# Local attention of a decoder trunk: one narrow split product for the meta keys, exponentials as a step of their own, output projection opened with three of four operand tiles

## The chip, the cores and the metric

The kernel runs on one NeuronCore of a Trainium2 chip. The core has five engines with a queue each: PE (TensorE, matrix products; its weight loads are listed apart as PEld), DVE (VectorE), ACT (ScalarE), POOL (GpSimd) and SP (which here issues transfers from memory). PE writes its results to eight banks of PSUM; everything else lives in SBUF, 128 partitions wide. The metric is the device time of one execution in microseconds (us); less is better.

## The reference

Two layers over 512 tokens and 16 meta tokens ahead of them, 1024 wide, all in float32. Layer 0 mixes by gated linear attention, layer 1 by local attention; each mixer stands between two half-step feed-forward nets, and each of these parts between two RMS norms. The change touches the local attention of layer 1, cut here to what matters:

```python
def swa_mixer(hn, w_q, sinks, w_out, k, v, cos, sin):
    q = (hn @ w_q).reshape(B, L, N_KV_HEADS, GROUP, HEAD_DIM)          # 4 key heads x 4, 64 wide
    q = apply_partial_rope(q, cos, sin) * (HEAD_DIM ** -0.5)
    ...
    k_band, v_band = band(k), band(v)       # per block of 128: 16 meta keys, the block before, the block itself
    s = jnp.einsum('bkgnqd,bknsd->bkgnqs', q_blk, k_band)
    mask = [meta: always, block before: j > i and blk > 0, own block: j <= i]
    p = sink_softmax(s, mask, sink_b)       # the sink adds exp(sink - max) to the denominator
    o_real = jnp.einsum('bkgnqs,bknsd->bkgnqd', p, v_band)
    ...
    return o @ w_out
...
hn = rmsnorm(h, g[2]); mix = swa_mixer(...); h = h + rmsnorm(mix, g[3])
```

The keys and values are made once, after layer 0, and shared (`shared_kv`). The meta positions are dropped from the output.

## The kernel before, in words

All activations are kept transposed: 1024 features as 8 tiles of 128 partitions, tokens along the free axis, in two groups of 256 (`L1`) or all 512 at once (`L1W`). Weights come from memory as plain float32 in 256 KB pieces and are split on chip: ACT copies a tile to the type fp32r (high part), DVE subtracts that copy from the original (low part). A product of two split operands is three products, high x high, low x high, high x low (`mm3s`, lines 348 to 359). A product of unsplit float32 operands is one instruction in the program and two records in the trace. `pair` tiles (32 slots of 2 x 528 elements per partition) hold weights, operands and most intermediates.

**Order.** The order of PE is the order in which the program calls it, and that is written by a small planner, `Flow` (lines 75 to 127). It keeps a clock that each product advances by an estimate (`mm`, line 175: columns/2400 us for split operands, columns/600 for plain ones). Jobs are generators; what they yield is a delay in planner time or another job to wait for. After a split product with a pump (`flow.pump()` in `mm3s`) all jobs that are due emit their instructions. With four outputs at once, as in `x_first`, the pumps stand at the last four of each twelve products; with one output, behind every third. The delays are constants at the top of the file.

**Local attention** (`swa`, from line 1250). One visit handles a pair of heads over two query blocks; 16 visits (`visits`) run as two jobs each. `soft(i)`: score products `sa` and `sb` for 4 (head, block) pairs, copy to SBUF (ACT, L1328), masked insertion of the block before (DVE, L1330), the sink's column (L1346), maximum (L1347), its scaling (L1348), four exponentials with row sums (ACT, L1350); after `SOFT` the reciprocal (L1355), the 16 meta weights of both heads scaled into `mt` (L1360) and the 128 others scaled in place (L1363). `core(i)`: `NORM` later two transposes of `mt` (`ptm`), copied to the tile `pm` (L1376), and four of the others (`pt`, L1384 and L1386); `PROBS` later the output bank `o`: one plain float32 product for the meta keys over 32 rows (two heads x 16), then products of 64 x 128 for the others (`vt`, `dv`); then `split` into the operand tile `so[u]` (L451, L452). `pace` keeps visits at least `PERIOD` (first eight) or `SLOWER` apart, and visit i waits for the core of visit i - 5.

Between the visits PE runs work from outside them: the second half of the query projection (`x`), and the output projection (`y`, `out_steps`, from line 666). The latter runs in two halves of four operand tiles `so`; for each group of 256 tokens and each of 8 output tiles `begin` makes the products with the first three operand tiles and `unit` adds the fourth and hands the bank on. For the second group it first waits for the visits of that group (`second`).

**Behind the attention**, `Residual.run` (per group): after a delay plus `sums[gi]` the sums of squares go through `root` on PE and DVE (`st_post`), after `DCHAIN` plus `factors[gi]` a product spreads the factors over the partitions (`r_post`, from the tile `dg_post`, L426), and DVE and ACT add the residual and build the next operand's tiles (L525, L526, L474, L475). The next net starts with `x_first`: four weight tiles at once, 96 products for group 0, then 96 for group 1, tile by tile as they are built. `fin` for the attention is made at line 1530.

**Shared values** (`shared_kv`, from line 1198): `place` transposes V into `vt`, forms the differences `dv` and the two tiles `vmz`, which hold the 16 meta rows of two value heads, each zero in the other head's rows (`rowm` is the 0/1 mask).

Of the kernel before, what the change touches and what calls it, by code (L numbers as in the profile page):

```python
# [11 lines left out]
I32 = mybir.dt.int32  # L12
# [31 lines left out]
SCORE = 0.8  # L44
SOFT = 6.5
ADDED = 1.4
LONGER = 0.8
BEHIND = 2.2
NORM = 4.0
BUSY = 2.6  # L50
# [5 lines left out]
SQUARES = 6.0  # L56
SLACK = 1.0
LAG = 5
PERIOD = 3.1
SLOWER = 3.6  # L60
GATHER = 1.5
# [77 lines left out]
def trunk_kernel(ctx: ExitStack, tc, a, out, last_out):  # L139
# [21 lines left out]
    def pair_tile(name, dt=F32R):  # L161
        return hp.tile([P, 2, TOK], dt, tag="pair", name=name)
# [5 lines left out]
    def flat(t):  # L168
        return t.rearrange("p a t -> p (a t)")
# [496 lines left out]
    def out_steps(hid, groups, split_groups, first, finish=None, tailm=0, packed=False, jobs=(), second=(), late=1):  # L666
# [80 lines left out]
        for gi, g in enumerate(split_groups):  # L747
            if gi:
                flow.wait(*second)
            for m in range(KD - tailm, KD):  # L750
                if finish and finish.turned(gi) and m == KD - 2:
                    hold(KD - 1, g)
                unit(m, g)
                if finish:
                    sq(m, gi)
                if gi:
                    done_w(through(m) - freed)
                    freed = through(m)
            if finish:
                flow.spawn(finish.run(gi, g, accs[gi]))  # L760
# [437 lines left out]
    def shared_kv(x, kp, behind):  # L1198
        kz = [kp.tile([P, 4, META + P], F32, name=f"kz{j}") for j in range(2)]
        vt = flat(pair_tile("vt", F32))[:, :1024].rearrange("p (b v) -> p b v", v=256)  # L1200
        dv = flat(pair_tile("dv", F32))[:, :768].rearrange("p (b v) -> p b v", v=256)
        vmz = [t[:, :P] for t in duo("vmz")]
        rowm = kp.tile([P, 8], F32, name="rowm")
        sp.dma_start(rowm, a["rowmask"])
# [16 lines left out]
        def place(drained):  # L1221
# [3 lines left out]
            for j in range(2):  # L1225
# [9 lines left out]
                vm = duo(f"vm{j}")[0]  # L1235
                dve.tensor_copy(vm[:, :32].rearrange("p (e m) -> p e m", m=META), v[:, :META].unsqueeze(1).to_broadcast([P, 2, META]))
                yield 1.0
                p = ps(f"vmT{j}")
                transpose(p[:32, :P], vm[:, :32])
                for e in range(2):  # L1240
                    d = slice(64 * e, 64 * e + 64)
                    dve.tensor_tensor(vmz[j][:32, d], p[:32, d], rowm[:32, e : e + 1].to_broadcast([32, 64]), op=ALU.mult)
                yield 1.0
            dve.tensor_tensor(dv, vt[:, 1:], vt[:, :3], op=ALU.subtract)

        job = flow.spawn(place(x_first(x, 4, evac, behind=behind, first_ahead=6)))
        return (kz, vt, dv, vmz), job


    def swa(x, kv, finish):  # L1250
        kz, vt, dv, vmz = kv
        cap[0] = used[0] + 8
        with tc.tile_pool(name="ap", bufs=1) as ap:
            mgt = ap.tile([P, P], I32, name="mgt")
            sp.dma_start(mgt, a["mgt"])
            mle = ap.tile([P, P], F32, name="mle")
            sp.dma_start(mle, a["mle"])
# [4 lines left out]
            sp.dma_start(sr, a["sinp"])  # L1262
            sel = ap.tile([P, 32], F32, name="sel")
            sp.dma_start(sel, a["sel"])
# [42 lines left out]
            def soft(i, after_jobs):  # L1307
# [39 lines left out]
                dve.tensor_reduce(nm, s, axis=AX.X, op=ALU.max, negate=True)  # L1347
                dve.tensor_tensor(pairs(nm), pairs(nm), both(rc), op=ALU.mult)  # L1348
                for c in range(4):
                    act.activation(  # L1350
                        s[:, c], s[:, c], AF.Exp, scale=rc[:, c % 2 : c % 2 + 1], bias=nm[:, c : c + 1],
                        accum_out=den[:, c : c + 1],
                    )
# [3 lines left out]

                mt = sm.tile([P, 2, 2, META], F32, tag="mt", name=f"mt{u}_{hf}", bufs=3)
                pairs = lambda t: t.rearrange("p (e c) m -> p e c m", c=2)
                dve.tensor_tensor(  # L1360
                    mt.rearrange("p c e m -> p e c m"), pairs(s[:, :, :META]), pairs(rd.to_broadcast([P, 4, META])), op=ALU.mult
                )
                dve.tensor_tensor(s[:, :, META:144], s[:, :, META:144], rd.to_broadcast([P, 4, P]), op=ALU.mult)  # L1363
                probs[i] = s, mt

            def core(i):
# [6 lines left out]
                for c in range(2):  # L1373
                    transpose(pm[:32, c * P : (c + 1) * P], mt[:, c].rearrange("p e m -> p (e m)"))
                ptm = sm.tile([32, 256], F32, tag="ptm", name=f"pm{u}_{hf}", bufs=2)
                act.activation(ptm, pm[:32, :256], AF.Copy)  # L1376
                p = ps(f"pt{u}_{hf}")
# [12 lines left out]
                kvh = [slice((2 * j + e) * 64, (2 * j + e) * 64 + 64) for e in range(2)]  # L1390
                mm(o[:, :256], vmz[j][:32], ptm, True, True)
                for c in range(2):
# [119 lines left out]
    with tc.tile_pool(name="kp", bufs=1) as kp:  # L1512
# [17 lines left out]
        nxt, fin = into("l1f1", 1, 3, False, lambda k: gain(1, 4, k), L1, post=(2, 2))  # L1530
        fin.sums[0] = SLACK
        flow.wait(placed)
# [18 lines left out]
def _layout(x, meta_tokens, norm_gains, w_ffn_in, w_ffn_out, gla_w_in, gla_w_gate, gla_b_gate, gla_norm,  # L1551
# [75 lines left out]
```

## Time and profile before

| | |
|---|---|
| median of 3 runs | 1878.34 us (1878.25 to 1880.12) |
| profiled execution, its own time | 1879.77 us |
| its span, first to last instruction | 1878.0 us |
| mean granted clock of TensorE | 0.998 |
| PE, PEld busy | 1867.2, 1786.4 us |
| DVE, ACT, POOL busy | 1398.1, 1026.7, 164.1 us |
| local attention, first score product to the last o product | about 1393 to 1498 us |

Times in rows are from the start of the span. A row of a group of instructions gives line, engine, operation, `out<-in` by tile names, partitions x elements and type; count; behind the bar busy us and mean ns of one; behind the second bar the idle time of the engine just before them and what ended it. A row in order of time gives start, length, engine, line and operation, merged over equal neighbours, with idle time in brackets. Matmul records overlap in their tails, so the cost of one is read from start to start. A row of the view of stretches gives busy time and instruction count of each engine, then the granted clock (1.00 is full speed), the share of the 16 DMA engines and GB/s.

### The profile page before, as it was taken

The page shows a single profiled execution, that of the slowest core. Times are in us where ns is not written, and L with a number is a line of the kernel's source. Part 1 is how long each engine was busy: PE and PEld are TensorE (multiplying, and loading weights), DVE is VectorE, ACT ScalarE, POOL GpSimd, SP SyncE. Part 2 cuts the span into 40 slices and gives each one's busy share as a digit, 9 for nine tenths or more (in the row PEclk, how much of TensorE's full clock was granted, in tenths as well). Part 3 has the DMA queues.
Part 4 walks back from the last instruction along what each step waited for, and adds up shares of the span by engine and source line. Part 5 has one row for each costly group of instructions (what it writes and reads, how often), then busy time and mean ns, then how long its engine had stood idle before and what let it go on. Part 6 is the DMA issues. An engine that isn't in the chain of part 4 may idle for free.

```text
span 1878.0 us, 37247 instructions
## 1 busy us (share of the span) xinstructions
PE 1867.2 (99%) x14463; PEld 1786.4 (95%) x14463; DVE 1398.1 (74%) x2837; ACT 1026.7 (55%) x2309; POOL 164.1 (9%) x295
## 2 busy tenths in 40 slices
PE   9999999999999999999999999999999999999998
PEld 9999999999999999999999898989988898989898
DVE  7885858767564788585887886868777679858685
ACT  5663635654446566363674553535767756636364
POOL 2000000330001300000033000000320140000002
PEclk9999999999999999999999999999999999999999
DMA  5233333421213123232351223233421212333331
GB/s 175 95 97 99 93 105 96 138 69 57 66 60 113 46 91 105 88 105 92 103 174 46 73 86 112 92 111 98 140 74 52 69 46 73 101 103 104 102 113 60
DMA packets 102274, 174.70 MB, mean 93 GB/s; under 512 B 11857, under 2 KB 24017, under 8 KB 102097
## 3 DMA queue, kind: packets, MB, share of 16 engines
q1 hardware_dynamic: 101664, 171.74, 28.8%
q8 instruction: 113, 1.85, 0.4%
q10 hardware_dynamic: 432, 0.59, 0.1%
q14 instruction: 65, 0.52, 0.1%
HBM read 169.66 MB, written 2.10 MB: 91 GB/s over the span
## 4 chain that ended last, share of the span: by engine, by line
PE 91%; DVE 6%; ACT 1%; issue 1%; DMA 0%; SPq 0%; DVEq 0%; ACTq 0%
PE y L176 31%; PE x L176 20%; PE a L176 19%; PE c L176 8%; PE d L176 5%; PE o L176 1%; DVE raw L265 1%; ACT w_s L259 1%; DVE w_s L260 1%; PE e L176 1%; DVE w L260 1%; PE po L176 1%; PE sa L176 1%; PE pt L188 1%; DVE w L241 1%
## 5 line engine op out<-in xcount | busy, mean ns | idle before, releaser
L260 DVE TENSOR_TENSOR w_s<-raw,w_s 128x512 fp32r<-128x512 f32 x288 | 193.9, 690 | 129.3 <-ACT w_s L259 127.2
L176 PE MATMUL y<-hidl0f,w 128*128 128x256 f32 (+1 forms) x2112 | 262.4, 285 | 1.1 <-DVE hidl0f L452 0.9
L176 PEld LDWEIGHTS y<-hidl0f,w 128*128 128x128 f32 x2112 | 259.3, 188 | 2.2 <-DVE hidl0f L452 1.5
L241 DVE TENSOR_TENSOR w<-raw,w 128x512 fp32r<-128x512 f32 x376 | 235.7, 655 | 30.1 <-ACT w L240 27.9
L259 ACT ACTIVATE w_s<-raw 128x512 fp32r<-128x512 f32 x288 | 175.1, 628 | 150.7 <-DVE raw L265 137.4
L176 PE MATMUL y<-hidl1f,w 128*128 128x512 f32 (+1 forms) x1344 | 251.1, 346 | 0.3
L176 PEld LDWEIGHTS y<-hidl1f,w 128*128 128x128 f32 x1344 | 212.4, 188 | 35.1 <-DVE hidl1f L941 1.5
L240 ACT ACTIVATE w<-raw 128x512 fp32r<-128x512 f32 x376 | 207.2, 586 | 39.8 <-PE y L176 29.9
L265 DVE TENSOR_TENSOR raw<-raw,raw 128x512 f32<-128x512 f32 x288 | 198.1, 688 | 5.5
L446 POOL TENSOR_TENSOR acc_post<-acc_post,sq_post 128x256 f32<-128x256 f32 (+1 forms) x77 | 62.6, 812 | 1532.4 <-ACT sq_post L445 1531.3
L260 DVE TENSOR_TENSOR w<-raw,w 128x512 fp32r<-128x512 f32 x216 | 148.4, 688 | 29.8 <-ACT w L259 29.0
L259 ACT ACTIVATE w<-raw 128x512 fp32r<-128x512 f32 x216 | 134.1, 621 | 41.6 <-PE y L176 41.0
L176 PE MATMUL x<-x_l0m,w 128*128 128x272 f32 (+1 forms) x1152 | 152.0, 288 | 0.0
L176 PEld LDWEIGHTS x<-x_l0m,w 128*128 128x128 f32 x1152 | 143.3, 188 | 2.7 <-issue 1.7
L705 DVE TENSOR_TENSOR Y<-y,Y 128x256 f32<-128x256 f32 (+2 forms) x175 | 82.0, 474 | 73.3 <-PE y L176 72.8
L176 PE MATMUL a<-zl0f_t,w_s 128*128 128x264 f32 x864 | 117.1, 285 | 0.0
L176 PE MATMUL a<-zl1f_t,w_s 128*128 128x256 f32 x864 | 114.7, 282 | 0.5 <-ACT c L916 0.4
L176 PEld LDWEIGHTS a<-zl0f_t,w_s 128*128 128x128 f32 x864 | 109.9, 188 | 0.3
L176 PEld LDWEIGHTS a<-zl1f_t,w_s 128*128 128x128 f32 x864 | 107.4, 188 | 2.4 <-ACT c L916 2.0
L176 PE MATMUL x<-x_l0f,w 128*128 128x256 f32 (+1 forms) x768 | 98.0, 287 | 0.8 <-DVE w L241 0.8
L176 PEld LDWEIGHTS x<-x_l0f,w 128*128 128x128 f32 x768 | 94.9, 188 | 2.0 <-DVE w L241 1.5
L176 PE MATMUL x<-x_l1f,w 128*128 128x256 f32 (+1 forms) x576 | 94.4, 323 | 0.0
(513 smaller groups left out, 3221.1 us busy)
## 6 DMA issues: line engine op xcount, KB each, us to landing
raw<-in_w_in SPq DMA_DIRECT2D x352, 256.0 KB, 2.9
raw<-in_w_out SPq DMA_DIRECT2D x96, 256.0 KB, 3.2
raw<-in_w_last SPq DMA_DIRECT2D x48, 256.0 KB, 3.1
raw<-in_gla_in SPq DMA_DIRECT2D x48, 256.0 KB, 3.2
raw<-in_w_out SPq DMA_DIRECT2D x64, 128.0 KB, 2.8
raw<-in_gla_out SPq DMA_DIRECT2D x16, 256.0 KB, 2.8
raw<-in_w_q SPq DMA_DIRECT2D x16, 256.0 KB, 4.5
raw<-in_swa_out SPq DMA_DIRECT2D x16, 256.0 KB, 3.0
```

The lines of the kernel that those rows point to most:

```text
L176: inst = pe.matmul(o, lhs, rhs, start=start, stop=stop, skip_group_check=onto)
L188: pe.transpose(o, src, ident)
L240: act.activation(w[:, 0, :m], raw[:, :m], AF.Copy)
L241: dve.tensor_tensor(w[:, 1, :m], raw[:, :m], w[:, 0, :m].bitcast(F32), op=ALU.subtract)
L259: act.activation(w[:, 0, :512], src, AF.Copy)
L260: dve.tensor_tensor(w[:, 1, :512], src, w[:, 0, :512].bitcast(F32), op=ALU.subtract)
L265: dve.tensor_tensor(dst, dst, src, op=ALU.add)
L446: pool.tensor_tensor(sums[0][:, :n], sums[0][:, :n], t[:, :n], op=ALU.add)
L705: dve.tensor_tensor(y, p[:, :n], y, op=ALU.add)
```

## The change

- The meta product becomes one split product over 96 rows. `mt` grows from 2 x 32 to 3 x 32 columns per block: the third part is first the plain weight (`mf`), ACT copies it to the first two parts as fp32r (high), and after `HIGH` DVE turns the third into the low part. The transposes `ptm` give 96 rows instead of 32, copied to an fp32r tile. On the value side `vmz` gets 96 rows: high, low, high (built in `place`, with the mask of two columns).
- The exponentials are issued `LARGEST` = 1.5 after the maximum; `SOFT` goes from 6.5 to 4.6, `NORM` from 4.0 to 2.5 with `HIGH` = 1.5 ahead of it.
- `PERIOD` 3.1 to 2.8, `SLOWER` 3.6 to 3.1.
- In the output projection of the attention, `begin` is called for the first two output tiles of each group before the first is finished (`OPENED`; only where `second` is given).
- Behind the attention `sums[0]` = 1.0 is dropped and `factors[1]` = 1.8 (`CROWDED`) set.
- The tables `mgt`, `mle` and `sel` move from a pool of their own into the unused end of the tile that holds `dv`.

```diff
-SOFT = 6.5
+LARGEST = 1.5
+SOFT = 4.6
...
-NORM = 4.0
+HIGH = 1.5
+NORM = 2.5
...
+OPENED = 2
+CROWDED = 1.8
 LAG = 5
-PERIOD = 3.1
-SLOWER = 3.6
+PERIOD = 2.8
+SLOWER = 3.1
...
             if gi:
                 flow.wait(*second)
+
+            for m in range(KD - tailm, KD - tailm + (OPENED if second else 0)):
+                begin(m, g)
             for m in range(KD - tailm, KD):
...
-        dv = flat(pair_tile("dv", F32))[:, :768].rearrange("p (b v) -> p b v", v=256)
-        vmz = [t[:, :P] for t in duo("vmz")]
-        rowm = kp.tile([P, 8], F32, name="rowm")
+        dv = flat(pair_tile("dv", F32))
+        dv, spare = dv[:, :768].rearrange("p (b v) -> p b v", v=256), dv[:, 768:]
+        both = pair_tile("vmz")
+        vmz = [both[:, j, :P] for j in range(2)]
+        rowm = kp.tile([P, 2], F32, name="rowm")
...
-                dve.tensor_copy(vm[:, :32].rearrange("p (e m) -> p e m", m=META), v[:, :META].unsqueeze(1).to_broadcast([P, 2, META]))
+                dve.tensor_copy(vm[:, :96].rearrange("p (e m) -> p e m", m=META), v[:, :META].unsqueeze(1).to_broadcast([P, 6, META]))
                 yield 1.0
                 p = ps(f"vmT{j}")
-                transpose(p[:32, :P], vm[:, :32])
+
+                transpose(p[:96, :P], vm[:, :96])
+                zm = duo(f"zm{j}")[0][:96, :P]
                 for e in range(2):
                     d = slice(64 * e, 64 * e + 64)
-                    dve.tensor_tensor(vmz[j][:32, d], p[:32, d], rowm[:32, e : e + 1].to_broadcast([32, 64]), op=ALU.mult)
+                    dve.tensor_tensor(zm[:, d], p[:96, d], rowm[:96, e : e + 1].to_broadcast([96, 64]), op=ALU.mult)
+                act.activation(vmz[j][:96], zm, AF.Copy)
+                dve.tensor_tensor(vmz[j][32:64], zm[32:64], vmz[j][32:64].bitcast(F32), op=ALU.subtract)
...
-            mgt = ap.tile([P, P], I32, name="mgt")
+            mgt = spare[:, :P].bitcast(I32)
             sp.dma_start(mgt, a["mgt"])
-            mle = ap.tile([P, P], F32, name="mle")
+            mle = spare[:, P : 2 * P]
             sp.dma_start(mle, a["mle"])
...
-            sel = ap.tile([P, 32], F32, name="sel")
+            sel = spare[:, 2 * P :]
             sp.dma_start(sel, a["sel"])
...
                 dve.tensor_tensor(pairs(nm), pairs(nm), both(rc), op=ALU.mult)
+
+                yield LARGEST
                 for c in range(4):
                     act.activation(
                         s[:, c], s[:, c], AF.Exp, scale=rc[:, c % 2 : c % 2 + 1], bias=nm[:, c : c + 1],
...
-                mt = sm.tile([P, 2, 2, META], F32, tag="mt", name=f"mt{u}_{hf}", bufs=3)
+                mt = sm.tile([P, 2, 3, 32], F32R, tag="mt", name=f"mt{u}_{hf}", bufs=3)
                 pairs = lambda t: t.rearrange("p (e c) m -> p e c m", c=2)
+                mf = mt[:, :, 2].bitcast(F32)
                 dve.tensor_tensor(
-                    mt.rearrange("p c e m -> p e c m"), pairs(s[:, :, :META]), pairs(rd.to_broadcast([P, 4, META])), op=ALU.mult
+                    mf.rearrange("p c (e m) -> p e c m", m=META), pairs(s[:, :, :META]), pairs(rd.to_broadcast([P, 4, META])), op=ALU.mult
                 )
+                act.activation(mt[:, :, :2], mf.unsqueeze(2).to_broadcast([P, 2, 2, 32]), AF.Copy)
                 dve.tensor_tensor(s[:, :, META:144], s[:, :, META:144], rd.to_broadcast([P, 4, P]), op=ALU.mult)
+                yield HIGH
+                dve.tensor_tensor(mt[:, :, 2], mf, mt[:, :, 0].bitcast(F32), op=ALU.subtract)
                 probs[i] = s, mt
...
-                    transpose(pm[:32, c * P : (c + 1) * P], mt[:, c].rearrange("p e m -> p (e m)"))
-                ptm = sm.tile([32, 256], F32, tag="ptm", name=f"pm{u}_{hf}", bufs=2)
-                act.activation(ptm, pm[:32, :256], AF.Copy)
+                    transpose(pm[:96, c * P : (c + 1) * P], mt[:, c].bitcast(F32).rearrange("p r k -> p (r k)"))
+                ptm = sm.tile([96, 256], F32R, tag="ptm", name=f"pm{u}_{hf}", bufs=2)
+                act.activation(ptm, pm[:96, :256], AF.Copy)
...
-                mm(o[:, :256], vmz[j][:32], ptm, True, True)
+                mm(o[:, :256], vmz[j][:96], ptm, True, True)
...
-        fin.sums[0] = SLACK
+        fin.factors[1] = CROWDED
         flow.wait(placed)
         swa(x, kv, fin)
...
-    c["rowmask"] = (i // META == np.arange(8)[None, :]).astype(np.float32)
+    c["rowmask"] = (i // META % 2 == np.arange(2)[None, :]).astype(np.float32)
```

More of the change, by code (lines that the diff above doesn't have):

```diff
@@ L1246, in shared_kv @@
         job = flow.spawn(place(x_first(x, 4, evac, behind=behind, first_ahead=6)))
-        return (kz, vt, dv, vmz), job
+        return (kz, vt, dv, vmz, spare), job
     def swa(x, kv, finish):
-        kz, vt, dv, vmz = kv
+        kz, vt, dv, vmz, spare = kv
         cap[0] = used[0] + 8
         with tc.tile_pool(name="ap", bufs=1) as ap:
-            mgt = ap.tile([P, P], I32, name="mgt")
+            mgt = spare[:, :P].bitcast(I32)
             sp.dma_start(mgt, a["mgt"])
-            mle = ap.tile([P, P], F32, name="mle")
+            mle = spare[:, P : 2 * P]
             sp.dma_start(mle, a["mle"])
```

## The prediction

> **What bounds the kernel now.** I read the page first, then who waited for whom, then the stretch that the change touches.
>
> ```profile
> PE 1867.2 (99%) x14463; PEld 1786.4 (95%) x14463; DVE 1398.1 (74%) x2837; ACT 1026.7 (55%) x2309; POOL 164.1 (9%) x295
> PE 91%; DVE 6%; ACT 1%; issue 1%; DMA 0%; SPq 0%; DVEq 0%; ACTq 0%
> ```
>
> PE is busy for 99% of the span and is 91% of the chain that ended last: time is won by giving PE less to do or by closing one of its few gaps. The view of waits for PE names the gaps, longest first:
>
> ```profile
> PE r_post_l1f L176 <- DVE dg_post_l1f L426: 2.0, 1, 2.0
> PE busy L1442 <- DVE eps L1494: 1.0, 1, 1.0
> ```
>
> The longest, 2.0 us, lies just behind the local attention. Inside it there is none, by busy time in its stretch (columns: us, then PE, PEld, DVE, ACT, POOL busy with counts, clock, DMA share, GB/s):
>
> ```profile
> 1400.00:1498.00 98.00, 98.00 (x877) 80.90 (x875) 69.85 (x186) 77.53 (x245) 4.75 (x6) 1.00 0.21 65
> ```
>
> So a product made cheaper here pays in full as long as ACT (77.5 of 98) and DVE (69.9) keep up.
>
> **The meta product.** PE in order of time (start, length, line, operation, count):
>
> ```profile
> 1443.39 3.44 PE L176 MATMUL y<-so,w 128*128 128x256 f32 x27
> 1446.77 0.69 PE L176 MATMUL o<-pm,vmz 32*128 32x256 f32 x2
> 1447.39 0.44 PE L176 MATMUL o<-pt,vt 128*64 128x128 f32 x4
> ...
> 1449.33 4.18 PE L176 MATMUL y<-so,w 128*128 128x256 f32 x33
> 1453.35 0.38 PE L188 MATMUL ptm<-ident,mt 128*32 128x128 f32 x2
> ...
> 1455.01 2.04 PE L176 MATMUL y<-so,w 128*128 128x256 f32 x15
> 1456.88 0.38 PE L188 MATMUL ptm<-ident,mt 128*32 128x128 f32 x2
> ```
>
> The product over the 16 meta keys is plain f32 and stands as two records: 1447.39 - 1446.77 = 0.62 us from its start to the next. A split (fp32r) product of the same 256 columns is a y: 33 of them take 4.02 (1449.33 to 1453.35) and 15 take 1.87, so one costs (4.02 - 1.87)/18 = 0.119 and the entry into such a block about 0.09. The block of 27 ends in a plain product and takes 3.38, 0.08 more than 27 x 0.119 + 0.09: leaving the block costs 0.08, and the change only shifts that behind the meta product. So where the meta product follows a split one it saves 0.62 - 0.119 = 0.50. In the timeline 12 of the 16 do (as here; the first of them at 1422.21, the last at 1496.42); the other 4 follow transposes or score products and would need entry and exit of their own: 0.50 - 0.17 = 0.33. Sum: 12 x 0.50 + 4 x 0.33 = **7.3 us**. Bounds for what the trace does not show, a split product over 96 rows: no gain at all if it costs what the plain one does (0), and 16 x 0.50 = 8.0. I take 7.3, since the y product has the same columns and 128 rows.
>
> The Trainium skill (FP8 and Floating Point Precision, TensorE Precision Notes) counts true fp32 as four passes through the array. As an estimate from that, three passes of 0.119 are saved, 0.36 a product and 5.7 in all in place of 7.3; the trace has 0.62 in two records, more than four such passes, so the row decides.
>
> The transposes that feed it load 96 columns instead of 32:
>
> ```profile
> 1433.84 0.38 PE L188 MATMUL ptm<-ident,mt 128*32 128x128 f32 x2
> 1434.06 0.60 PE L188 MATMUL pt<-ident,s 128*128 128x128 f32 x4
> 1434.41 1.67 PE L176 MATMUL y<-so,w 128*128 128x256 f32 x12
> ```
>
> Two with 32 columns take 0.22, four with 128 take 0.35: about 0.1 each either way, so 96 columns cost nothing.
>
> **What ACT and DVE get in return.** Groups of the stretch 1400 to 1498:
>
> ```profile
> L1350 ACT ACTIVATE s<-s,nm,roots 128x145 f32<-128x145 f32 x48 | 23.8, 498 | 8.3 <-DVE nm L1348 8.2
> L1376 ACT ACTIVATE pm<-ptm 32x256 f32<-32x256 f32 x16 | 5.8, 363 | 1.7 <-PE ptm L188 1.7
> L1384 ACT ACTIVATE pt<-pt 128x512 f32<-128x512 f32 x16 | 9.3, 580 | 0.2
> L445 ACT ACTIVATE sq_post<-Y 128x256 f32<-128x256 f32 x6 | 2.4, 410 | 1.5 <-DVE Y L705 1.5
> L1360 DVE TENSOR_TENSOR mt<-s,den 128x64 f32<-128x64 f32 x12 | 2.7, 227 | 0.3
> ```
>
> New on ACT is one copy of 128 elements a visit. From 256 to 512 elements a copy grows by 580 - 363 = 217 ns, so 128 fewer than L445's 256 is 410 - 109 = 0.30 us; bounds half of L445's and all of it, 0.2 and 0.41. 16 x 0.30 = 4.8 us. New on DVE is one subtraction of 64 elements: by L1360 0.23, at most twice that, 16 x 0.23 = 3.7. The stretch shrinks to 98 - 7.3 = 90.7; ACT then has 82.3 (91%), DVE 73.6 (81%). Against that, ACT stood idle for 8.2 us ahead of L1350, the exponentials at the head of its queue waiting for the maximum of their own visit; issued 1.5 later in the planner's time, they let other copies go ahead. Two waits are new: ACT's copy for DVE's weights, behind which the next copies of scores and transposes queue, and DVE's subtraction for that copy, behind which the next maximum and the weight splits queue; the 1.5 ahead of the subtraction is longer than the copy's 0.30. Cover for the additions is that idle time; without it, 4.8 is what ACT falls behind. I book 0.5 us for one gap as small as those already in the list of waits, between 0 and 3.
>
> **Pace.** Visits start 0.3 (later 0.5) sooner after one another, and from exponentials to transposes the plan goes from 6.5 + 4.0 = 10.5 to 1.5 + 4.6 + 1.5 + 2.5 = 10.1. The tightest visit I found:
>
> ```profile
> 1431.38 0.68 DVE L1363 TENSOR_TENSOR s<-s,den 128x512 f32<-128x512 f32 x1
> ```
>
> The scaled weights are there at 1432.06, their transposes run at 1434.06: 2.0 to spare, against 0.4 less plan and 0.23 more DVE. Cost 0.
>
> **Edits at nothing.** Two tiles opened with three of four operands: the order of 9 products changes, not their number; a second bank is held some 9 x 0.119 = 1.1 us longer. The row below (1498.07) shows no wait there to remove. The table loads leave their own pool for the spare end of dv:
>
> ```profile
> L1255 SPq DMA_DIRECT2D mgt<-in_mgt x1: 328/328/328, 17.1 to 17.1; - x1
> L1264 SPq DMA_DIRECT2D sel<-in_sel x1: 861/861/861, 18.4 to 18.4; - x1
> ```
>
> They now go out 17 us into the kernel, where their place was free; in a slot that others use first they can't, so these three issues (0.33, as much again for mle, and 0.86: 1.5 us on SP) move late in SP's queue, past most weight loads, and what is queued behind them waits for that slot. Weights lie ahead in a ring, so I book 0, at most 1.5. Preparing the wider meta values adds two small copies on ACT and some four subtractions or wider multiplications' worth on DVE, about 0.6 and 0.9 us, in a stretch with room and PE full:
>
> ```profile
> 1025.00:1040.00 15.00, 15.00 (x93) 13.19 (x92) 11.44 (x27) 4.23 (x9) 0.00 (x0) 1.00 0.00 1
> ```
>
> **Behind the attention.** The residual of group 0 loses a delay of 1.0 ahead of its sums, group 1 gains 1.8 ahead of its factor product r_post.
>
> ```profile
> 1498.07 4.17 PE L176 MATMUL y<-so,w 128*128 128x256 f32 x33
> 1502.08 0.95 PE L176 MATMUL st_post_l1f<-ones,acc_post 128*128 128x1 f32 x8
> ...
> 1515.09 0.95 PE L176 MATMUL st_post_l1f<-ones,acc_post 128*128 128x1 f32 x8
> 1515.90 4.47 PE L176 MATMUL x<-x_l1f,w 128*128 128x256 f32 x36
> 1522.38 0.70 PE L176 MATMUL r_post_l1f<-dg_post_l1f,ones 128*128 128x256 f32 x2 [2.00 <-DVE dg_post_l1f L426]
> ...
> 1533.65 7.74 PE L176 MATMUL x<-x_l1f,w 128*128 128x256 f32 x57
> ```
>
> ```profile
> 1521.91 0.42 DVE L426 TENSOR_TENSOR dg_post_l1f<-ident,yv_post_l1f 128x256 f32<-128x256 f32 x1
> ...
> 1536.87 0.48 DVE L475 SCALAR_TENSOR_TENSOR x_l1f<-H,vec,x_l1f 128x256 fp32r<-128x256 f32 x1
> ```
>
> PE stands from 1520.38 to 1522.38, until DVE has dg. The gap costs twice, by the clock (PE alone, then all engines over the whole place):
>
> ```profile
> 1515.00:1520.00 5.00, 5.00 (x46) 1.00 0.01 3
> 1523.00:1527.20 4.20, 4.20 (x25) 0.59 0.38 124
> ```
>
> ```profile
> 1511.20:1525.00 13.80, 11.80 (x95) 11.54 (x94) 12.55 (x36) 8.18 (x21) 6.94 (x9) 0.96 0.10 32
> ```
>
> After it the granted clock is 0.59 for 4.2 us: another 0.41 x 4.2 = 1.7, so 3.7 in all. The planner counts 256/2400 = 0.107 a product, so 1.8 is 17 products more; it looks up only at the last four of each twelve, which by the counts makes it twelve, 1.4 us. A delay of 1.0 less in group 0 starts its work on DVE some nine products sooner, which frees DVE for dg by up to 1.0. 2.0 - 1.4 - 1.0 is below nothing: the gap closes. What is late next is the last operand tile of group 1, done on DVE at 1537.35. Of 96 products for that group 51 lie behind 1533.65, and the tile's low half is first read by the 48th: 1533.65 + 47 x 0.119 = 1539.2. It has 1.9 to spare, and r_post itself now runs 0.6 sooner (1520.38 + 1.4 = 1521.8): of the 3.7 about **2.5 us** can be had. Bounds 0 (the wait only moves) and 3.7.
>
> The Trainium skill (TensorE: Matmul & The Clock Gate, Part 1: The HAM clock gate) has the clock halved after an idle window of some 3.4 us, which a gap of 2.0 doesn't fill. By that the edit would be worth 2.0 at most, 0.5 less in the sum; here the clock did fall behind a gap of 2.0.
>
> **Sum.** -7.3 - 2.5 + 0.5 = -9.3. The profiled execution took 1879.77 (span 1878.0 and 1.77 around it), which gives 1870.5; the median of the runs shown lies 1.43 lower, so 1878.34 - 9.3 = **1869.0 us**.
>
> **Rivals.**
> 1. The tail gives nothing: r_post is later, and group 1's tiles are late by as much. For it: DVE is busy for 12.55 of 13.8 us there, so what it makes comes when it comes, and the last tile has only 1.9 to spare. Against: the 1.9. 1878.34 - 7.3 + 0.5 = 1871.5.
> 2. **ACT becomes the bound**, and the kernel slower. Place: the visits, 1400 to 1498. ACT has 98 - 77.5 = 20.5 us idle there; only 8.2 of it is the wait that the change addresses, and the new copy adds a round trip DVE, ACT, DVE to each visit. If all 20.5 stays, the stretch is 82.3 + 20.5 = 102.8 long, 4.8 more than now, and two gaps of the 2 us kind add 2 x 1.7 in clock: 1878.34 + 4.8 + 3.4 - 2.5 = 1884.0. It eats the gain from an idle time of 90.7 - 82.3 = 8.4 us on and turns the sign at about 18. Against: 2.0 us and more of room before PE needs a result.
> 3. One new gap as long as today's in the denser stretch, with its clock: 2.0 + 1.7 in place of the 0.5: 1872.2. For it: 2.0 at the tightest visit, and a bank held longer.
> 4. The product gets no cheaper: 96 rows as a split product cost what the plain one does (the trace has no such product, the nearest is y). 1878.34 - 2.5 + 0.5 = 1876.3.
>
> **How the numbers follow.** Forecast 0.58, rival 1 0.13, rival 3 0.11, rival 4 0.09, rival 2 0.09. About 0.2%, 3.8 us, is what a measurement of this kernel can tell from no change. Forecast, 1 and 3 lie below 1874.6: faster 0.82, less 0.02 for their upper ends, 0.80. Rival 4 and those ends lie within: 0.11. Rival 2: 0.09. The low end is 8.0 + 3.7 gained and no new gap, 1866.6, and half a microsecond for another order of blocks: 1866. The high end takes in rivals 1 and 3 and most of rival 4: 1876.
>
> **What would show it.** Right: the meta product stands as one record of about 0.12 to the next start, 16 in all; PE full from the first visit to r_post; no wait of r_post for dg, clock 1.00 behind it; ACT at about 0.9 in the visits. Wrong: idle time of PE ahead of transposes or o products, released by ACT or DVE; a wait of x for DVE L475 as long as the one removed; SP standing at the loads of mgt, mle and sel with weights behind them.

## The result, and the profile after

Measured: **1882.3 us** median of 21 runs (1880.41 to 1884.21) against 1879.21 (21 runs, 1877.88 to 1880.18). The ratio is 1.0016, with a 95% interval of 1.0011 to 1.0022: slower by about 3 us, just inside the 0.2% that counted as no change. The forecast was 1869.0 (1866 to 1876) and faster.

The page of after, engine totals and the shares of the chain that ended last:

```profile
span 1878.5 us, 37253 instructions
PE 1861.6 (99%) x14447; PEld 1783.4 (95%) x14447; DVE 1397.7 (74%) x2855; ACT 1029.3 (55%) x2327; POOL 163.3 (9%) x295
PE 83%; DVE 10%; ACT 4%; issue 2%; DMA 0%; SPq 0%; DVEq 0%; ACTq 0%
```

PE is busy for 5.6 us less, idle for 6.1 more (1878.5 - 1861.6 = 16.9 against 1878.0 - 1867.2 = 10.8), and the span is 0.5 longer: work was saved, and PE stood for longer than that. Its share of the chain fell from 91% to 83%, and DVE and ACT took the difference. Who PE waited for, in after from 1388 to 1545 (us in total, times, longest):

```profile
PE x L180 <- ACT x_l1f L478: 2.3, 2, 1.8
PE sa L180 <- ACT s L1341: 1.3, 1, 1.3
PE o L180 <- DVE pt L1405: 0.8, 2, 0.6
PE ptm L192 <- DVE mt L1382: 0.8, 1, 0.8
PE x L180 <- DVE x_l1f L479: 0.8, 1, 0.8
PE o L180 <- ACT pm L1395: 0.6, 1, 0.6
PE o L180 <- ACT s L1341: 0.4, 2, 0.2
```

The wait of r_post for dg (2.0) is gone. Two others stand in its place: x for the operand tiles of group 1, 2.3 + 0.8 = 3.1, behind the attention; and scores, transposes and o products inside the visits, where before had none. (Lines are shifted by the diff: products L176 is L180, transposes L188 is L192, score copies are L1341, masking L1343, maximum L1360, exponentials L1365, operand tiles L478 and L479.) The stretch of the visits in after, all engines:

```profile
1400.00:1498.00 98.00, 93.83 (x870) 80.65 (x869) 71.31 (x202) 80.82 (x263) 4.91 (x6) 1.00 0.21 66
```

PE was busy for all 98.00 before. ACT's load went from 77.53 to 80.82 only, far from full. What ACT waited for in after, 1388 to 1512:

```profile
ACT s L1365 <- DVE nm L1361: 12.6, 10, 1.9
...
ACT Y L1365 <- DVE nm L1361: 1.9, 2, 1.2
```

Its exponentials stand for the maximum of their own visit for 14.5 us; in before the same two rows (s and Y) hold 8.2 + 1.8 = 10.0. The idle time that was to make room for the new work grew. PE at two of the gaps, in order of time (the gap and its releaser in brackets), with the first meta products:

```profile
1420.22 0.38 PE L180 MATMUL o<-pm,vmz 96*128 96x256 f32 x1
1420.54 0.66 PE L180 MATMUL o<-pt,vt 128*64 128x128 f32 x8
...
1422.75 0.80 PE L180 MATMUL sa<-kz,q 64*128 64x144 f32 x4 [1.34 <-ACT s L1341]
...
1429.69 0.40 PE L192 MATMUL ptm<-ident,mt 128*96 128x128 f32 x2 [0.77 <-DVE mt L1382]
...
1430.28 0.95 PE L180 MATMUL y<-so,w 128*128 128x256 f32 x6
1431.07 0.28 PE L180 MATMUL o<-pm,vmz 96*128 96x256 f32 x1
1431.28 0.44 PE L180 MATMUL o<-pt,vt 128*64 128x128 f32 x4
```

The meta product is one record now and takes 1431.28 - 1431.07 = 0.21 to the next start. ACT ahead of the first gap, and then DVE:

```profile
1418.19 0.31 ACT L1379 ACTIVATE mt<-mt 128x128 fp32r<-128x128 f32 x1
1420.33 0.51 ACT L1365 ACTIVATE s<-s,nm,roots 128x145 f32<-128x145 f32 x1 [1.83 <-DVE nm L1361]
...
1422.31 0.68 ACT L1341 ACTIVATE s<-sa 128x288 f32<-128x288 f32 x2
```

```profile
1416.73 0.18 DVE L1370 RECIPROCAL den<-den 128x4 f32<-128x4 f32 x1 [2.23 <-ACT s L1365]
...
1417.41 0.78 DVE L1343 COPY_PREDICATED s<-dv,sb 128x256 f32<-128x256 int32 x2 [0.25 <-ACT s L1341]
...
1419.09 0.74 DVE L1360 TENSOR_REDUCE nm<-s 128x4 f32<-128x580 f32 x1
```

From 1418.50 ACT does nothing for 1.83 us, because the exponentials next in its order wait for DVE's maximum; the copy that would free PE's score bank comes behind them at 1422.31, and PE waits for it. DVE in its turn had stood 2.23 for the exponentials of the visit before. The two engines wait for each other, and what I call the turn below is one round of this: exponentials, score copies, masking, maximum, exponentials. So at this gap, the longest of the visits, ACT is idle first and late afterwards.

Behind the attention, PE of after:

```profile
1514.93 5.91 PE L180 MATMUL x<-x_l1f,w 128*128 128x256 f32 x48
1520.68 0.50 PE L180 MATMUL st_l1f<-ones,acc_l1f 128*128 128x1 f32 x4
1521.04 0.68 PE L180 MATMUL r_post_l1f<-dg_post_l1f,ones 128*128 128x256 f32 x2
...
1534.30 1.20 PE L180 MATMUL x<-x_l1f,w 128*128 128x256 f32 x8 [1.84 <-ACT x_l1f L478]
1536.26 0.74 PE L180 MATMUL x<-x_l1f,w 128*128 128x256 f32 x4 [0.75 <-DVE x_l1f L479]
1537.46 4.47 PE L180 MATMUL x<-x_l1f,w 128*128 128x256 f32 x24 [0.46 <-ACT x_l1f L478]
```

and DVE of after there:

```profile
1517.98 0.43 DVE L430 TENSOR_TENSOR dg_post_l1f<-ident,yv_post_l1f 128x256 f32<-128x256 f32 x1
1521.76 0.43 DVE L529 TENSOR_TENSOR r_post_l1f<-Y,r_post_l1f 128x256 f32<-128x256 f32 x1 [3.35 <-PE r_post_l1f L180]
...
1535.25 0.41 DVE L782 TENSOR_TENSOR gu<-x,R_l1f 128x256 f32<-128x256 f32 x1
...
1537.44 0.48 DVE L479 SCALAR_TENSOR_TENSOR x_l1f<-H,vec,x_l1f 128x256 fp32r<-128x256 f32 x1 [0.25 <-ACT x_l1f L478]
```

48 products now run ahead of r_post where 36 did: the twelve that the delay was worked out to be. But dg is there at 1518.41, so r_post, at 1521.04, is late for no reason, and DVE stands for 3.35 us. The group's tiles then meet group 0's first evacuations (L782) and weight splits on DVE and are ready last at 1537.92.

### The profile page after: what moved, and what is told of

Same layout as the page of the kernel before. It is cut to its first block, busy times and chain, and to the rows that moved or that the text cites. A ratio compares the mean times of both kernels' runs of the same rounds, so it can differ in the third digit from the quotient of the medians.

```text
span 1878.5 us, 37253 instructions
## 1 busy us (share of the span) xinstructions
PE 1861.6 (99%) x14447; PEld 1783.4 (95%) x14447; DVE 1397.7 (74%) x2855; ACT 1029.3 (55%) x2327; POOL 163.3 (9%) x295
## 4 chain that ended last, share of the span: by engine, by line
PE 83%; DVE 10%; ACT 4%; issue 2%; DMA 0%; SPq 0%; DVEq 0%; ACTq 0%
PE y L180 29%; PE a L180 18%; PE x L180 18%; PE c L180 8%; PE d L180 4%; DVE raw L269 2%; ACT w_s L263 1%; ACT s L1365 1%; DVE w_s L264 1%; DVE w L264 1%; DVE w L245 1%; PE e L180 1%; PE po L180 1%; DVE nm L1360 0%; DVE hidl1f L948 0%
## 5 line engine op out<-in xcount | busy, mean ns | idle before, releaser
L180 PE MATMUL y<-hidl0f,w 128*128 128x256 f32 (+1 forms) x2112 | 262.4, 285 | 1.1 <-DVE hidl0f L456 0.8
L180 PEld LDWEIGHTS y<-hidl0f,w 128*128 128x128 f32 x2112 | 259.3, 188 | 2.2 <-DVE hidl0f L456 1.5
L180 PE MATMUL y<-hidl1f,w 128*128 128x512 f32 (+1 forms) x1344 | 251.7, 346 | 0.8 <-DVE hidl1f L456 0.4
L180 PEld LDWEIGHTS y<-hidl1f,w 128*128 128x128 f32 x1344 | 212.3, 188 | 36.2 <-DVE hidl1f L948 1.6
L180 PE MATMUL x<-x_l0m,w 128*128 128x272 f32 (+1 forms) x1152 | 152.0, 288 | 0.0
L180 PEld LDWEIGHTS x<-x_l0m,w 128*128 128x128 f32 x1152 | 143.3, 188 | 2.7 <-issue 1.7
L180 PE MATMUL a<-zl0f_t,w_s 128*128 128x264 f32 x864 | 117.2, 285 | 0.0
L180 PE MATMUL a<-zl1f_t,w_s 128*128 128x256 f32 x864 | 114.6, 282 | 1.1 <-ACT c L923 0.5
L180 PEld LDWEIGHTS a<-zl1f_t,w_s 128*128 128x128 f32 x864 | 107.4, 188 | 3.0 <-ACT c L923 2.0
L180 PEld LDWEIGHTS a<-zl0f_t,w_s 128*128 128x128 f32 x864 | 110.0, 188 | 0.3
L180 PE MATMUL x<-x_l0f,w 128*128 128x256 f32 (+1 forms) x768 | 98.1, 287 | 0.9 <-ACT w L244 0.4
L180 PEld LDWEIGHTS x<-x_l0f,w 128*128 128x128 f32 x768 | 94.8, 188 | 2.3 <-DVE w L245 1.3
L180 PE MATMUL x<-x_l1f,w 128*128 128x256 f32 (+1 forms) x576 | 93.9, 321 | 3.1 <-ACT x_l1f L478 2.3
```

Source lines behind the costliest of these rows:

```text
L180: inst = pe.matmul(o, lhs, rhs, start=start, stop=stop, skip_group_check=onto)
```

## The experiments

The rows suggest two things: the delay of 1.8 costs the tail, and the turn between ACT and DVE holds up the visits. What theory A and theory B stand for, and the rival of each run, is said anew in each expectation. Each time is a median, each ratio is against the kernel before on the same chip (1878.67 or 1878.68).

**The delay taken away** (after, without the 1.8).

```
-        fin.factors[1] = CROWDED
         flow.wait(placed)
```

> The changed kernel with the delay of 1.8 ahead of group 1's factor product taken out again (factors[1] = 0), nothing else. In the changed kernel's profile dg is ready at 1518.41 us and r_post, its only reader, runs at 1521.04; DVE stands idle for 3.35 us until then, and PE waits 1.84 + 0.75 + 0.46 = 3.05 us later for the last operand tiles. Theory A (the delay is what made the tail late): r_post about 1.4 to 2.6 us sooner, the 3.05 us of waits fall below 1, and the time falls by 2 to 4 us to about 1879. Theory B (the last tiles are late because DVE and ACT have the evacuations of group 0 and the weight splits ahead of them, whatever r_post does): waits stay near 3 us and the time stays within 1 us of 1882.3. My prediction's own step says r_post would then wait 0 to 1.4 us for dg.

1875.46, ratio 0.9982 (0.9973 to 0.9991): 6.8 below after by the medians, 6.4 by the two ratios. PE, and then DVE, of this kernel:

```profile
1514.71 4.50 PE L180 MATMUL x<-x_l1f,w 128*128 128x256 f32 x36
1519.05 0.59 PE L180 MATMUL r_post_l1f<-dg_post_l1f,ones 128*128 128x256 f32 x2
...
1527.25 9.16 PE L180 MATMUL x<-x_l1f,w 128*128 128x256 f32 x69
```

```profile
1519.68 0.43 DVE L529 TENSOR_TENSOR r_post_l1f<-Y,r_post_l1f 128x256 f32<-128x256 f32 x1 [1.50 <-PE r_post_l1f L180]
...
1532.73 0.63 DVE L479 SCALAR_TENSOR_TENSOR x_l1f<-H,vec,x_l1f 128x256 fp32r<-128x256 f32 x1
```

r_post runs 2.0 sooner, the last tile is ready 4.6 sooner (1533.36 against 1537.92), and no x waits. The delay alone turned a gain into a loss. It costs more than the 3.05 us of its gaps. Between the two profiled executions, both at clock 1.00, the spans differ by 5.6 (1878.5 and 1872.9). The next stage's first y product starts 4.1 later in after (1562.56 against 1558.47), of which 0.2 was there ahead of the tail (group 1's statistics at 1514.13 against 1513.90). Two waits in that stage that this kernel doesn't have, shown under "The sum", make it 5.3 (1589.03 against 1583.69). The rest of the 6.4 to 6.8 may be clock: after's runs range over 3.8 us and mostly lengthen as their clock falls (1880.4 to 1880.5 at 1.000, up to 1884.2 at 0.997), and here all eleven are at 1.000 or 0.999. That fits and isn't shown.

**The tail's two edits alone** (before, without the 1.0, with 1.8).

```
-        fin.sums[0] = SLACK
+        fin.factors[1] = 1.8
```

> The kernel before with the change behind the attention alone: the 1.0 ahead of group 0's sums dropped, 1.8 ahead of group 1's factor product. Prediction as recorded: the 2.0 us gap and the clock drop behind it go, 2.5 us faster, 1876.7 beside 1879.2. Theory A: group 0's work on DVE ends sooner, so dg comes sooner and r_post, later by 12 products, leaves DVE idle; the wait moves to the last operand tiles: same or up to 3 us slower, with PE waiting for tiles built at the end of group 1.

1878.63, ratio 0.9999 (0.9991 to 1.0008). The gap at r_post closed (2.0 to 0.07), as I had worked out, and nothing was won: x waits 0.47 for a tile, and the products behind group 1's statistics start 0.45 later (1516.35 against 1515.90). My 2.5 is not there even in the kernel for which I worked it out: the interval ends at 0.9991, 1.7 us.

**The dropped 1.0 put back, no 1.8** (after).

```
-        fin.factors[1] = CROWDED
+        fin.sums[0] = 1.0
```

> The changed kernel with the tail of before: the 1.0 ahead of group 0's sums back, the 1.8 ahead of group 1's product gone. If the dropped 1.0 is what lets group 1 have DVE early, this loses against the first run (1875.5): about 1 to 3.7 us slower, with r_post waiting for dg and the clock falling behind the gap as before. If the 1.0 is worth nothing, the same as the first run within 1 us.

1875.73, ratio 0.9982 (0.9973 to 0.9991), as without it: the 1.0 is worth nothing, and r_post hardly waits for dg here either (0.07). So dg's lateness of 2.0 was gone from the changed kernel before the tail's edits touched it.

**The product alone** (before's pace, joined exponentials at 6.5, no opening, before's tail).

```
-PERIOD = 2.8
-SLOWER = 3.1
-SOFT = 4.6
-OPENED = 2
+PERIOD = 3.1
+SLOWER = 3.6
+SOFT = 6.5
+OPENED = 0
...
-                yield LARGEST
```

> The meta product as one split product (with its copies, the step of 1.5 ahead of the low part, and the tables in dv's spare end) and nothing else of the change: pace, exponentials, opening and tail as before. If the cheaper product pays in full, PE's time in the visits falls by 5.5 us (that is what the 16 product records of the changed kernel take less) and the time by 5 to 6, to about 1874. If the copies on ACT and the round trip between DVE and ACT are what PE waits for, PE shows gaps in the visits as in the changed kernel (4.2 us) and the time falls by 1 to 2 only. If the gaps come from the pace, there are none here.

1879.44, ratio 1.0001 (0.9992 to 1.001): nothing won. PE stands for 6.8 us in its visits (the sum of its gaps), the longest:

```profile
1423.19 0.80 PE L180 MATMUL sa<-kz,q 64*128 64x144 f32 x4 [1.34 <-ACT s L1341]
...
1432.31 2.18 PE L180 MATMUL y<-so,w 128*128 128x256 f32 x16 [2.02 <-DVE so L456]
```

The gaps are there without the new pace, the new step and the opening: the product, with its copy and its subtraction, is enough to open them. Whether it is the shorter part of PE or the work added to ACT and DVE, the doubled copy below has to say.

**Before's pace in after** (PERIOD 3.1, SLOWER 3.6).

> The changed kernel with the pace of before (3.1 and 3.6 instead of 2.8 and 3.1), nothing else. If the denser visits are what lets PE overtake ACT and DVE, the gaps of 4.2 us in the visits fall below 1.5 and the time falls by about 3 to 1879, with the 3.05 us of the tail left. If ACT's and DVE's added work is the cause, the gaps stay near 4 and the time within 1 us of 1882.3.

1890.06, ratio 1.0057 (1.0044 to 1.0071): 7.8 above after, which neither expectation had. The shorter plan isn't the cause of the gaps: with before's pace PE stands 8.0 us from the first scores to the statistics of group 0 (2.02 for so, 1.70 ahead of transposes and 1.37 ahead of the statistics among them), in place of 4.2. I had booked 0. But the 7.8 isn't the price of the pace alone. The profiled execution's span is 10.3 longer than after's (1888.8 against 1878.5), and three stretches at a lower clock, shown in the last section, are about 5.1 of that.

**The opening taken away** (from the kernel without the delay, OPENED = 0).

> The changed kernel without the delay of 1.8 and without opening two output tiles ahead. Prediction as recorded: worth nothing, within 1 us of 1875.5. Rival: the earlier end of the visits' work makes PE ask for the fourth operand tile sooner than it is split, and the opening covers that: 1 to 3 us slower without it, with PE waiting for so.

1879.81, ratio 1.0002 (0.9993 to 1.0011): 4.3 above the kernel without the delay. PE stands 7.1 us in the visits in place of 4.2, and y waits for so, 2.02 at 1432.28, where the kernel with the opening has no such gap. Another 1.7 of the profiled execution is clock behind that gap (last section).

**The exponentials joined to the masking again** (from the kernel without the delay).

```
-SOFT = 4.6
+SOFT = 6.1
...
-                yield LARGEST
```

> The changed kernel without the delay of 1.8 (as in the first run, 1875.5 us) and with the exponentials issued together with the maximum again (the step of 1.5 gone, the rest of the plan kept: 6.1 from there to the weights). In the run without the delay ACT still stands idle for 12.6 + 1.9 us ahead of the exponentials, more than the 10.0 of before. Theory A (the step of 1.5 is too short to bring another visit's score copies ahead of the exponentials, so it does nothing): the idle time stays between 10 and 16 us and the time within 1.5 us of 1875.5. Theory B (my prediction's: the step lets copies go ahead): without it ACT idles longer, PE's gaps of 4.2 us in the visits grow and the time rises by 2 or more.

1877.51, ratio 0.9994 (0.9985 to 1.0003): the step is worth 2.0, and without it PE stands 5.7 us in the visits instead of 4.2. But ACT's wait for the maximum is nearly as long with it as without (14.5 against 13.1 + 1.9). The step helps, though not by giving ACT its idle time back, which was the way I gave.

**ACT's new copy made twice** (from the kernel without the delay).

```
+                for _ in range(2):
                     act.activation(mt[:, :, :2], mf.unsqueeze(2).to_broadcast([P, 2, 2, 32]), AF.Copy)
```

> The changed kernel without the delay of 1.8 (1875.5 us) and with ACT's new copy of 128 elements made twice in every visit (16 more copies of 0.31 us). If the visits are bound by ACT and DVE waiting for each other, each extra copy that stands in that turn lengthens it: PE's gaps in the visits grow from 4.2 us by 2 to 5 and the time rises by 2 to 5. If ACT has room (it is busy for 87 of 105 us), the extra copies disappear: within 1 us of 1875.5.

1875.44, ratio 0.9983 (0.9974 to 0.9992): free. Sixteen more copies change nothing, PE's idle time in the visits stays 4.2, and ACT's wait for the maximum shrinks to 10.9 + 1.1. PE's wait for the subtraction behind the copy grows, from 0.78 to 0.97, without costing time. So ACT is not short of time, and the added copy is not what holds up the visits.

**The exponentials issued later still** (from the kernel without the delay).

```
-LARGEST = 1.5
+LARGEST = 3.5
-SOFT = 4.6
+SOFT = 3.4
```

> The changed kernel without the delay of 1.8 and with the exponentials 3.5 behind the maximum instead of 1.5, weights 3.4 behind them. Theory A (in the visits ACT and DVE wait for each other in turn: exponentials, then the next visit's score copies on ACT, then masking, maximum on DVE, then again exponentials, about 5.7 us a turn, more than PE now needs for a visit): with the next visit's copies ahead of the exponentials the turn is broken, ACT idles less than 6 us ahead of them, PE's gaps in the visits fall from 4.2 to below 2 and the time falls by 2 to 4, to 1872 to 1873.5. Theory B (the gaps are ACT's and DVE's sheer load): no change within 1.5 us, or slower because the weights come later for the transposes.

**1873.94**, ratio 0.9971 (0.9959 to 0.9982): below both kernels. ACT's waits in it:

```profile
ACT s L1365 <- DVE nm L1361: 6.5, 7, 1.7
...
ACT Y L1365 <- DVE nm L1361: 1.1, 2, 0.7
```

14.5 became 7.6, and PE's idle time in the visits fell from 4.2 to 1.7 with no work removed. So when the exponentials are issued decides about the gaps, and not how much ACT has to do. That they stood too early ahead of copies that PE wants is the reading of the gap shown above; the run doesn't isolate it, since the same edit puts the transposes 0.8 later in the plan (10.9 in place of 10.1 behind the maximum) and PE's own order changes with the planner's clock. PE's waits in it, 1388 to 1545:

```profile
PE r_post_l1f L180 <- DVE dg_post_l1f L430: 1.7, 2, 1.5
PE turn L180 <- ACT q L1284: 0.7, 1, 0.7
PE o L180 <- DVE so L456: 0.5, 1, 0.5
```

With the visits faster, dg is late again: of 2.5 won in the visits, 1.5 reach the end.

**The same with the plain product** (before, with pace, opening, a step of 3.5 and no 1.0).

```
-SOFT = 6.5
+LARGEST = 3.5
+SOFT = 3.4
+OPENED = 2
-PERIOD = 3.1
-SLOWER = 3.6
+PERIOD = 2.8
+SLOWER = 3.1
...
-        fin.sums[0] = SLACK
```

> The kernel before with the new pace, the opening of two output tiles, the exponentials 3.5 behind the maximum and the 1.0 dropped, but with the plain meta product of 0.62 us: the run with late exponentials (1873.9 us) less the product. If the product pays now that the turn between ACT and DVE is broken, this is 4 to 5.5 us slower than that run, about 1878 to 1879, and PE's visits have no gaps. If the visits are still bound by ACT and DVE, which have less to do here, it is within 1.5 us of 1873.9.

1881.22, ratio 1.0011 (1.0002 to 1.002). Against the run above the split product, with its copy and subtraction, is worth 1881.22 - 1873.94 = 7.3 us. This kernel is 2.5 slower than before. Part of that is PE's own work: from the first scores to the last y it takes 124.4 us with the gaps of 1.35 taken out (1389.15 to 1514.85), against 122.4 in before, and half of the 2.0 more are the products `turn` (1426.65 to 1428.67, in before 1424.55 to 1425.54). Why these take longer in this order stays open. The run also bounds what ACT's idle time tells: ACT stands for the maximum for 12.8 + 1.3 us here, as long as in after, and PE waits for only 1.35.

**Later again, and a half delay.** From the kernel without the delay, LARGEST 4.5, SOFT 3.4, HIGH 1.0 and NORM 2.0; and from the one with 3.5 and 3.4, a delay of 0.9 ahead of r_post.

> As the run with late exponentials, but 4.5 behind the maximum, with 3.4, 1.0 and 2.0 behind that (10.9 in all, as there). If the rest of ACT's idle time ahead of the exponentials (7.6 us there) goes with more distance, PE's gaps of 1.7 us in the visits go too: up to 2 us faster than 1873.9. If the weights now come too late for their transposes, PE waits for DVE ahead of them: 1 to 4 us slower.

> The run with late exponentials (1873.9 us), in which r_post waits 1.47 us for dg again, with a delay of 0.9 ahead of it, half of the change's. The planner looks up only at the last four of each twelve products, so 0.9 moves r_post by a whole twelve (1.4 us) or not at all. If it moves and dg's time is unchanged, the gap closes: PE gains up to 1.4 us if the operand tiles of group 1 have that much to spare, and loses up to 3 if they have not. I expect within 1.5 us of 1873.9, and the runs of the changed kernel say rather slower.

The first took 1875.07, ratio 0.9979 (0.997 to 0.9988), 1.1 above 3.5 and 3.4: y waits 1.4 for so, so results seem to come too late now. The second took 1873.85, ratio 0.9972 (0.9962 to 0.9983): r_post stayed where it was (gap 1.35), and by the planner, which moves it by whole groups of twelve products, a delay of less than a group can move nothing.

## Why the prediction was wrong, step by step

**The meta product** was priced nearly right. One record, 0.21 to 0.23 behind a y where PE didn't wait (predicted 0.119 and 0.08 of leaving the block: 0.20; the 0.12 given as a sign of being right left the 0.08 out) and 0.29 to 0.32 behind a transpose (predicted 0.119 + 0.17 = 0.29). From start to next start the 16 products took 10.0 before (32 records) and 4.5 after. The 5.5 saved there agrees with PE's own time in the visits, 5.4 less by the sum below, not with 7.3. I took before's order, 12 behind a split product; in after it is 8, and by my own prices that is 8 x 0.50 + 8 x 0.33 = 6.6; the other 1.1 stays unplaced. That the two runs with late exponentials, with the split product and with the plain one, differ by just 7.3 doesn't bear the sum out: their order of products is another one. The 96 columns cost nothing, as booked. Groups of after, 1390 to 1495, for the new work:

```profile
L1379 ACT ACTIVATE mt<-mt 128x128 fp32r<-128x128 f32 x16 | 4.9, 306 | 0.0
L1382 DVE TENSOR_TENSOR mt<-mt 128x64 fp32r<-128x64 f32 x16 | 3.8, 237 | 0.6 <-ACT mt L1379 0.6
```

0.31 and 0.24 each, where 0.30 and 0.23 were predicted. The Trainium skill (ScalarE: Activation LUTs, What ACT_TABLE_LOAD costs) gives 186 ns + 0.833 ns an element for an activation without pointer operands; as an estimate from that, 128 elements take 0.29, and the row, 306 ns, agrees within 5%.

**The first step that failed** is "issued 1.5 later in the planner's time, they let other copies go ahead", with "Cover for the additions is that idle time". I asked whether ACT and DVE had time, and they had: a second copy cost nothing. The question was how long a turn takes beside a visit. In before the score products of three visits start 6.27 and 6.23 apart (1406.99, 1413.26 and 1419.49), the exponentials 6.25 and 5.17 (1408.04, 1414.29 and 1419.46): the turn keeps up. In after the scores start 5.19 and 5.26 apart (1407.17, 1412.36 and 1417.62), but the exponentials 6.25 and 5.71 (1408.37, 1414.62 and 1420.33): the turn falls behind, and the next scores wait 1.34. Under before's own plan, in the run of the product alone, the exponentials stand 14.0 us for the maximum instead of 10.0 and PE stands 6.8; in after, where 0.5 of PE's waiting was booked, it is 4.2. A step of 1.5 was too little; with 3.5 it is 1.7. Rival 2 had the place right (the visits, ACT) but the wrong mechanism: it made ACT's load and the new copy's round trip the bound, and a doubled copy speaks against both.

**Pace and opening at nothing** were wrong on both sides. "2.0 to spare" was too much: the transposes' wait of 0.77 for the new subtraction is that edge. But undoing the pace costs 7.8 and undoing the opening 4.3, both with clock in them. The reason I gave for 0, no wait there to remove, held only as long as the product was dear; once PE waits, what feeds it earlier can pay. These prices are not additive, each having been taken with the others in place.

**The tail** is the larger error. "The gap closes" was right, and "of the 3.7 about 2.5 us can be had" became a loss of 6.4 to 6.8. I took dg's lateness from before's trace and left it fixed, though the edits ahead of it change when DVE is free; in after dg was 2.6 us early (1518.41 against 1521.04), and with before's tail in the changed kernel the lateness of 2.0 was already down to 0.07. And I priced only the way from r_post to the last tile, with 1.9 to spare, as if DVE's work between them stayed as it was. From r_post's start to the last tile it took 14.3 us without the delay (1519.05 to 1533.36) and 16.9 with it (1521.04 to 1537.92): more of the evacuations and weight splits of the next stage had moved in between. Rival 1 named that wait but bounded its harm at zero gain; a delay that nobody needs costs what it delays. The dropped 1.0, credited with up to 1.0 for dg, is worth nothing.

**The table loads** held: SP now stands at the first of them, and PE doesn't notice. This row of after is SP's wait:

```profile
SPq L1268 <- PE x L180: 16.6, 1, 16.6
```

SP stands for 16.6 us, until 1030.3, and no gap of PE follows, as booked.

**The sum.** Profile against profile: from the first scores to the last y PE takes 122.4 us in before (1388.82 to 1511.20) and 117.0 in after with its gaps taken out (1389.02 to 1510.21, less 4.2). This saving of 5.4 and the gaps of 4.2 leave -1.2 where -6.8 was forecast, and at the statistics of group 1 after is 1.0 ahead (1514.13 against 1515.09). Without before's gap of 2.0 and the clock lost behind it, after is 4.1 ahead once 48 more products and r_post are done (1521.37 against 1525.48). The tail's gaps of 3.05, and what PE loses in starting again behind each, take most of that: the next stage's y products start 0.8 sooner than in before (1562.56 against 1563.38). Two waits of PE in that stage, which before doesn't have, take the rest:

```profile
1567.81 17.87 PE L180 MATMUL y<-hidl1f,w 128*128 128x512 f32 x76 [0.41 <-DVE hidl1f L456]
...
1589.03 1.68 PE L180 MATMUL a<-zl1f_t,w_s 128*128 128x256 f32 x12 [0.40 <-ACT d L915]
```

At the second after is 0.3 behind (1589.03 against 1588.69), and its span ends 0.5 later. Without the delay neither wait is there, so they too belong to its price. The range was too narrow: it left out rival 2, at 1884.0, and no case let the delay in the tail cost more than it gains.

## What to carry to other kernels

When the bound engine's work in a loop gets cheaper, look at the turn between the other engines per iteration, and at what stands idle at the head of their queues, before looking at their loads: here the saving paid only once the exponentials were issued later for the shorter iteration. A delay that was fitted to a lateness in the old trace must be fitted again after every edit ahead of it, and the first thing to try is to leave it out. Price an edit in the kernel that has the others: here the same product was worth nothing alone and 7.3 us beside late exponentials, and the same delay, with the 1.0 dropped, was worth nothing in before and lost more than 6 us in after.

## What the runs showed of the hardware

A gap of 2.0 us on PE is followed by a lower clock in one execution and not in another. The same y product waited 2.02 us for so, at 1432.3, in the kernel without the opening and in the one with the product alone. Windows of the first, behind that gap:

```profile
1433.00:1435.00 2.00, 2.00 (x12) 1.78 (x10) 1.16 (x5) 2.00 (x9) 0.00 (x0) 0.50 0.26 56
1435.00:1437.00 2.00, 2.00 (x20) 1.83 (x19) 2.00 (x4) 1.54 (x5) 0.00 (x0) 0.66 0.23 54
```

and of the second:

```profile
1433.00:1437.20 4.20, 4.20 (x45) 3.89 (x44) 3.16 (x10) 3.61 (x14) 0.00 (x0) 1.00 0.30 67
```

0.50 and 0.66 against 1.00. The run with before's pace shows both in one execution. Behind its gap of 2.02 us, at 1432.33, the clock stays at 1.00; behind gaps of 1.70 (to 1491.12), 1.37 (to 1502.46) and 2.14 (to 1541.19) it falls:

```profile
1432.30:1436.50 4.20, 4.17 (x43) 3.86 (x43) 4.02 (x11) 4.19 (x16) 0.00 (x0) 1.00 0.21 45
1493.00:1497.00 4.00, 4.00 (x26) 3.67 (x27) 2.97 (x5) 2.42 (x8) 1.50 (x3) 0.57 0.10 38
1503.00:1508.00 5.00, 5.00 (x36) 4.54 (x36) 2.38 (x12) 0.38 (x1) 0.00 (x0) 0.66 0.02 3
1541.00:1545.00 4.00, 3.27 (x15) 2.98 (x16) 3.98 (x7) 3.94 (x10) 0.99 (x1) 0.57 0.54 164
```

Each of these losses is worth 1.7 us (0.43 x 4, 0.34 x 5 and 0.43 x 4), and so is the one in the kernel without the opening (0.50 x 2 + 0.34 x 2) and before's (0.41 x 4.2): whether it comes varies, what it costs didn't in these five. So the 1.7 that I charged before's gap for its clock belongs to that one execution; a single profile can't tell how often it is paid. The 29 executions of before that were timed beside the last experiments leave a hole between 1878.92 and 1879.53, with 17 below it and 12 above. The profiled one, 1879.77, lies above, and the median from which the forecast starts, 1878.34, below; that the lower ones had no such loss fits, and then those 1.7 were not there to be won from that median, but no profile of one was taken.

The Trainium skill (TensorE: Matmul & The Clock Gate, Part 1: The HAM clock gate) asks for an idle window of some 3.4 us before the clock halves, and says that the window runs free, so that the same kernel meets it differently from run to run. The second agrees with these rows; the first doesn't, since gaps of 2.0 us and less were enough here.
